# A softmax kernel: the split row moves to the first load, and three tiles become four

## The chip, the cores and the metric

One core of one Trainium2 chip. The metric is device time in microseconds (us) of one execution; the kernel before takes 160.3 us, the median of 5 runs (160.09 to 161.03).

## The reference

The input is 16 x 1024 rows of 512 float32 numbers, 33.55 MB; the output has the same size. Each row goes through a softmax at temperature 2:

```python
x_scaled = x / 2.0
x_max = np.max(x_scaled, axis=-1, keepdims=True)
exp_x = np.exp(x_scaled - x_max)
return exp_x / np.sum(exp_x, axis=-1, keepdims=True)
```

## The kernel before, in words

The 16,384 rows are laid on 128 partitions, so each partition has 128 rows of 2 KB. The text calls "a row" one such row on all 128 partitions (256 KB). The rows are cut into nine tiles, `TILES` (line 10): 3, 5, 15, 15, 25, 25, 10, 15 and 15 rows; each has a place in one buffer in on-chip memory, `arena`, which has room for 98 rows. Within a tile a partition's rows are contiguous in DRAM, so a transfer of r rows moves one piece of r x 2 KB per partition.

The fast path leaves out the row's maximum. ScalarE takes exp(0.5 x) in place, one row at a time, and the same instruction sums the row into `stats` (lines 204 and 271). VectorE takes the reciprocal of up to 15 sums (line 166) and multiplies up to 15 rows by theirs (line 169). At the end a count of sums in a safe range (lines 180 to 196) decides whether a slower path with the maximum must run after all; for these inputs it doesn't.

The order of the work is written out by hand, with a semaphore for each hand-over.

- Loads. `early()` (line 153) issues tile 0 on SyncE's queue and tile 1 on ScalarE's queue, ahead of the barrier at the program's start. After the barrier `loads()` (line 157) issues tiles 2 to 6 on ScalarE's queue, back to back: with tiles 0 and 1 these fill the 98 rows of `arena`.
- Late loads. The two last tiles (7 and 8) reuse rows of `arena` whose tiles have been stored. `LATE` names the tiles whose stores must have landed: 0, 1 and 2 for tile 7, and 3 for tile 8. GpSimd issues them (lines 176 to 179). Ahead of both it waits until the exponentials of all rows up to `TURN` = 63 are done.
- Stores. SyncE issues them in the order of the tiles (line 211), each when VectorE's multiplications of that tile are done (`store`, line 135).
- ScalarE takes rows in groups of 5 (`E`; the first group has 3, `HEAD`). TensorE passes on the landing of a tile (line 194) as so many groups in `s_go`, which ScalarE takes one by one (line 140).
- VectorE multiplies up to three groups at a time, in the last tile one group at a time (line 84).

`load()` (line 113) issues a tile as one transfer, except for the tile numbered `SPREAD`: its last row is loaded by itself, in one transfer over 126 partitions and one over the other 2. Tile `SPREAD` therefore has three transfers and a landing count of 48 instead of 16 (line 194). Before, that is tile 1, on ScalarE's queue.

Of the kernel before, what the change touches and what calls it, by code (L numbers as in the profile page):

```python
# [7 lines left out]


TILES = [  # L10
    (3, 0), (5, 3), (15, 8), (15, 23), (25, 38), (25, 63), (10, 88), (15, 0), (15, 15),
]

LATE = {7: (0, 1, 2), 8: (3,)}
ARENA = 98

HEAD = [3]
E = 5

SPREAD = 1  # L20

TURN = 63

LO, HI = 1.0, 1.0e30
G = 64
# [3 lines left out]
def kernel(  # L29
# [61 lines left out]
    ld = [nc.alloc_semaphore(f"ld{t}") for t in range(len(tiles))]  # L91
    s_home = {t: nc.alloc_semaphore(f"s_home{t}") for t in LATE}
    s_near = nc.alloc_semaphore("s_near")
# [19 lines left out]
    def load(eng, t):  # L113
        r = tiles[t][1]
        parts = [(0, P, 0, r)]
        if t == SPREAD:
            parts = [(0, P, 0, r - 1), (0, 126, r - 1, r), (126, P, r - 1, r)]
        for p, q, lo, hi in parts:
            eng.dma_start(  # L119
                out=sb(t)[p:q, lo:hi], in_=dram(xf, t)[p:q, lo:hi]  # L120
            ).then_inc(ld[t], 16)

    stored_by = {u: s_home[t] for t, us in LATE.items() for u in us}
    for t, (_, r, at) in enumerate(tiles):
        over = {u for u, (_, ru, au) in enumerate(tiles[:t]) if at < au + ru and au < at + r}
        assert over <= {u for v, us in LATE.items() if v <= t for u in us}

    def landings(ts):
        return 16 * len(list(ts))
# [27 lines left out]
    def loads():  # L157
        for t in range(2, min(LATE)):
            load(nc.scalar, t)

    def program():
# [13 lines left out]
        nc.gpsimd.memset(ones[:, :], 1.0).then_inc(s_ones, 1)  # L175
        nc.gpsimd.wait_ge(s_exp, starts.index(TURN))
        for t, us in LATE.items():
            nc.gpsimd.wait_ge(s_home[t], landings(us))
# [14 lines left out]
        for t in range(len(tiles)):  # L193
            nc.tensor.wait_ge(ld[t], 48 if t == SPREAD else 16).then_inc(s_go, owner.count(t))
        nc.tensor.wait_ge(s_ones, 1)
# [126 lines left out]
```

## Time and profile before

| | us |
|---|---|
| Median of 5 runs | 160.3 |
| The profiled execution, its own time | 160.91 |
| Its span, first to last instruction | 159.6 |
| ScalarE busy | 80.5 |
| VectorE busy | 73.3 |
| GpSimd busy | 2.2 |
| Loads of tile 0 issued / landed | 0.0 / 5.8 |
| First exponential | 6.36 |
| First and last store issued | 10.34 / 135.62 |
| Late loads issued | 67.77, 93.96 |

The span is what the profile's views cover; the profiled execution's own time has 1.3 us more, which lie around the span, and it was 0.6 us above the median. The 16 DMA engines of the core are shared by three queues: q1 is SyncE's (tile 0 and all stores), q10 ScalarE's (tiles 1 to 6), q0 GpSimd's (tiles 7 and 8). A packet is one piece of a transfer: one partition's share of a tile, and there is one small packet more for each DMA engine that reports the end of its part. In the windows view the DMA share is the time that the packets begun in a window took, over 16 engines; it may lie over 1, as a packet counts in full where it begins.

### The profile page before, as it was taken

To read this page: it belongs to the slowest core of one execution; us is meant where nothing else is said; L and a number is where in the kernel's file an instruction comes from. 1 tells how busy PE (TensorE), PEld (TensorE's weight loads), DVE (VectorE), ACT (ScalarE), POOL (GpSimd) and SP (SyncE) were. 2 spreads that over 40 slices of the span, in tenths; PEclk is the share of its full clock that TensorE was granted. 3 is DMA by queue.
4 is the path that set the end of the run, shared out by engine and by line. 5 is a ranking of instruction groups with operands and counts; after the bars stand their busy time and mean duration, and the time that the engine had idled before them with its cause. 6 is when DMAs were issued, how large, how long until landed. Compare 5 with 4: busy or idle time off the path is not lost. (4 is left out here: it accounts for less than half of the span.)

```text
span 159.6 us, 656 instructions
## 1 busy us (share of the span) xinstructions
PE 0.2 (0%) x2; PEld 0.1 (0%) x2; DVE 73.3 (46%) x29; ACT 80.5 (50%) x257; POOL 2.2 (1%) x8
## 2 busy tenths in 40 slices
PE   0000000000000000000000000000000000000000
PEld 0000000000000000000000000000000000000000
DVE  0056001992980009994007997019389599000000
ACT  0780498696003999401999700799911992000000
POOL 0000000000000000010000010000000001000000
DMA  6999998999789998989899997998999997999994
GB/s 264 385 493 414 444 440 346 516 493 447 318 352 452 441 521 352 511 352 459 377 488 403 459 485 336 441 503 344 467 413 449 411 500 336 475 431 454 408 454 185
DMA packets 2737, 67.11 MB, mean 421 GB/s; under 512 B 305, under 2 KB 305, under 8 KB 689
## 3 DMA queue, kind: packets, MB, share of 16 engines
q1 hardware_dynamic: 1440, 34.34, 50.1%
q10 hardware_dynamic: 1008, 24.90, 37.0%
q0 software_dynamic: 288, 7.86, 11.5%
q14 instruction: 1, 0.00, 0.0%
HBM read 33.55 MB, written 33.55 MB: 420 GB/s over the span
## 5 line engine op out<-in xcount | busy, mean ns | idle before, releaser
L271 ACT ACTIVATE arena<-arena x125 | 76.6, 614 | 46.9 <-ACTq L140 36.6
L169 DVE TENSOR_TENSOR arena<-arena,recip 128x7680 f32<-128x7680 f32 (+3 forms) x13 | 70.3, 5410 | 0.4
L166 DVE RECIPROCAL recip<-stats 128x15 f32<-128x15 f32 (+3 forms) x13 | 2.8, 217 | 62.2 <-ACT arena L271 53.8
L271 ACT ACTIVATION_READ_ACCUMULATOR arena<-arena x125 | 23.4, 187 | 0.0
L200 ACT ACT_TABLE_LOAD x1 | 1.3, 1283 | 5.1 <-issue 5.1
L119 POOL DMA_DIRECT2D arena<-in_x_dram x2 | 1.3, 632 | 90.5 <-DMA out_dram<-arena 90.5
L204 ACT ACTIVATE arena<-arena 128x512 f32<-128x512 f32 x3 | 1.9, 618 | 0.0
L180 POOL TENSOR_SCALAR inside<-stats 128x128 f32<-128x128 f32 x1 | 0.6, 631 | 38.1 <-ACT arena L271 38.1
L204 ACT ACTIVATION_READ_ACCUMULATOR arena<-arena 128x1 f32 x3 | 0.6, 187 | 0.0
L196 PE MATMUL total<-ones,count 128*1 128x1 f32 x2 | 0.2, 164 | 135.9 <-DVE inside L184 135.9
L184 DVE SCALAR_TENSOR_TENSOR inside<-inside,stats 128x128 f32<-128x128 f32 x1 | 0.3, 284 | 0.0
L188 DVE TENSOR_SCALAR flag<-total 1x1 int32<-1x1 f32 x1 | 0.1, 146 | 0.3 <-PE total L196 0.3
L196 PEld LDWEIGHTS total<-ones,count 128*1 128x1 f32 x2 | 0.1, 80 | 135.9 <-DVE inside L184 135.9
L175 POOL MEMSET ones<- 128x1 f32 x1 | 0.1, 99 | 2.2 <-POOLq L37 2.2
L306 POOL MEMSET const-float32-0.0<- 128x1 f32 x1 | 0.1, 105 | 0.2 <-issue 0.2
L306 POOL MEMSET const-bfloat16-1.0<- 128x1 bf16 x1 | 0.1, 108 | 0.0
L306 POOL MEMSET const-uint8-127<- 128x1 uint8 x1 | 0.1, 108 | 0.0
L306 POOL MEMSET const-float32-1.0<- 128x1 f32 x1 | 0.1, 105 | 0.0
L184 DVE DVE_READ_ACCUMULATOR inside<-inside,stats 128x1 f32 x1 | 0.1, 82 | 0.0
## 6 DMA issues: line engine op xcount, KB each, us to landing
out_dram<-arena SPq DMA_DIRECT2D x4, 3840.0 KB, 28.5
arena<-in_x_dram ACTq DMA_DIRECT2D x2, 6400.0 KB, 58.7
out_dram<-arena SPq DMA_DIRECT2D x2, 6400.0 KB, 40.7
arena<-in_x_dram ACTq DMA_DIRECT2D x2, 3840.0 KB, 20.5
arena<-in_x_dram POOLq DMA_DIRECT2D x2, 3840.0 KB, 29.9
arena<-in_x_dram ACTq DMA_DIRECT2D x1, 2560.0 KB, 96.0
out_dram<-arena SPq DMA_DIRECT2D x1, 2560.0 KB, 28.4
out_dram<-arena SPq DMA_DIRECT2D x1, 1280.0 KB, 28.3
```

Of the source, the lines that this page charges most:

```text
L119: eng.dma_start(out=sb(t)[p:q, lo:hi], in_=dram(xf, t)[p:q, lo:hi]).then_inc(ld[t], 16)
L166: nc.vector.reciprocal(out=recip[:, b : b + c], in_=stats[:, b : b + c])._wait_ge(s_exp, ks[-1] + 1).then_inc(s_rec, 1)
L169: nc.vector.tensor_mul(out=arena[:, a : a + c], in0=arena[:, a : a + c], in1=recip[:, b : b + c].unsqueeze(2).to_broadcast([P, c, D]),)._w ...
L175: nc.gpsimd.memset(ones[:, :], 1.0).then_inc(s_ones, 1)
L180: nc.gpsimd.tensor_scalar(out=inside[:, :], in0=stats[:, :], scalar1=LO, scalar2=HI, op0=Alu.max, op1=Alu.min,)._wait_ge(s_exp, len(sizes) ...
L184: nc.vector.scalar_tensor_tensor(out=inside[:, :], in0=inside[:, :], scalar=1.0, in1=stats[:, :], op0=Alu.mult, op1=Alu.is_equal, accum_ou ...
L188: nc.vector.tensor_scalar(out=flag[:, :], in0=total[:, :], scalar1=float(N), scalar2=None, op0=Alu.is_ge,)._wait_ge(s_tot, 1).then_inc(s_f ...
L196: nc.tensor.matmul(total[:, :], lhsT=count[:, :], rhs=ones[:, :], start=True, stop=True)._wait_ge(s_cnt, 2).then_inc(s_tot, 1)
L200: nc.scalar.preload_act_table(Exp)
L204: ins = nc.scalar.activation(out=arena[:, b], in_=arena[:, b], func=Exp, scale=0.5, accum_out=stats[:, b : b + 1],)
L271: ins = nc.scalar.activation(out=data, in_=data, func=Exp, scale=0.5, accum_out=stats[:, r : n_rows - E + 1 + r][:, bass.ds(now, 1)],)
L306: nc = _bacc.Bacc("TRN2", target_bir_lowering=False, num_devices=1)
```

## The change

- Tiles 4, 5 and 6 (25, 25 and 10 rows) become four tiles of 15 rows. There are now ten tiles: 3, 5 and eight times 15. The late tiles are numbers 8 and 9, with the same places in `arena` and the same stores to wait for.
- `SPREAD` is 0: the transfers over 126 and 2 partitions are now the third row of tile 0, on SyncE's queue, and tile 1 is one transfer.
- `TURN` is 83: GpSimd issues its loads after the exponentials of all rows up to 83.

```diff
 TILES = [
-    (3, 0), (5, 3), (15, 8), (15, 23), (25, 38), (25, 63), (10, 88), (15, 0), (15, 15),
+    (3, 0), (5, 3), (15, 8), (15, 23), (15, 38), (15, 53), (15, 68), (15, 83), (15, 0), (15, 15),
 ]
 
-LATE = {7: (0, 1, 2), 8: (3,)}
+LATE = {8: (0, 1, 2), 9: (3,)}
 ARENA = 98
 
 HEAD = [3]
 E = 5
 
-SPREAD = 1
-
-TURN = 63
+SPREAD = 0
+
+TURN = 83
```

## The prediction

> **What bounds the kernel now.** I read the page's totals first, then the DMA queues, then windows of the span, then who waits.
>
> ```profile
> span 159.6 us, 656 instructions
> PE 0.2 (0%) x2; PEld 0.1 (0%) x2; DVE 73.3 (46%) x29; ACT 80.5 (50%) x257; POOL 2.2 (1%) x8
> DMA packets 2737, 67.11 MB, mean 421 GB/s; under 512 B 305, under 2 KB 305, under 8 KB 689
> q1 hardware_dynamic: 1440, 34.34, 50.1%
> q10 hardware_dynamic: 1008, 24.90, 37.0%
> q0 software_dynamic: 288, 7.86, 11.5%
> ```
>
> No compute engine is busy more than half the time, while the three queues' packets took 50.1 + 37.0 + 11.5 = 98.6% of 16 engines' span, 157.4 us. The windows view (columns: length, busy time of PE, PEld, DVE, ACT and POOL, clock, DMA share, GB/s) says where the rest is:
>
> ```profile
> 0.00:1.00 1.00, 0.00 (x0) 0.00 (x0) 0.00 (x0) 0.00 (x0) 0.21 (x4) 1.00 0.00 0
> 1.00:2.00 1.00, 0.00 (x0) 0.00 (x0) 0.00 (x0) 0.00 (x0) 0.00 (x0) 1.00 0.70 246
> ...
> 8.00:156.00 148.00, 0.19 (x2) 0.09 (x2) 73.34 (x29) 77.61 (x252) 1.90 (x3) 1.00 1.01 432
> ...
> 157.50:158.00 0.50, 0.00 (x0) 0.00 (x0) 0.00 (x0) 0.00 (x0) 0.00 (x0) 1.00 0.30 123
> 158.00:158.50 0.50, 0.00 (x0) 0.00 (x0) 0.00 (x0) 0.00 (x0) 0.00 (x0) 1.00 0.14 61
> 158.50:159.00 0.50, 0.00 (x0) 0.00 (x0) 0.00 (x0) 0.00 (x0) 0.00 (x0) 1.00 0.00 0
> ```
>
> 1.3 us are empty at the start (1.0 + 0.3), nothing from 8 to 156, and 159.6 - 1.3 - 157.4 = 0.9 us at the end. At the end 123 GB/s x 0.5 us = 61 KB is two packets of 30,720 bytes and 61 x 0.5 one more: three of the 16 engines start their last packet up to 1 us after the others. So the time is start + packets + last landing, and a compute engine matters only if it lets the queues run dry.
>
> **Price of a packet.** Three windows of the DMA view hold one size each:
>
> ```profile
> q1 hardware_dynamic: 227, 5.99, 86.8%
> ...
> q1 hardware_dynamic: 91, 4.66, 107.6%
> ...
> q10 hardware_dynamic: 65, 0.13, 98.7%
> ```
>
> 144 to 160 us: 195 packets of 30,720 bytes (and 32 end packets) in 0.868 x 16 x 16 = 222 us, 1.138 us each. 120 to 130: 91 of 51,200 bytes in 172.2 us, 1.892 each. 6.05 to 6.40: 65 of 2048 bytes in 5.53 us, 0.085 each. From the two large sizes 1000 bytes cost 36.8 ns, so what doesn't grow with size is 1.138 - 1.131 = 7 ns in the one and 0.085 - 0.075 = 10 ns in the other: I take 8.5 ns. 4.194 MB and 171 packets per engine then make 154.4 + 1.5 = 155.9 us; the 157.4 hold 1.5 us in which packets took longer than their size explains.
>
> **The change, part by part.** *Four tiles of 15 for 25, 25 and 10.* The bytes stay. One load and one store more are 2 x 144 packets (128 pieces and 16 end packets), 18 per engine: 18 x 8.5 ns = +0.15 us. From below, the longer packets (51,200 bytes) might be what stalls: all 1.5 us gone is the end of that side. From above, the same 1.5 us might come again with more, shorter packets. No row ties these 1.5 us to a size: the windows of 12 us with 50 KB loads at work have 418 and 422 GB/s (32 to 56 us), the one from 128 to 140 404 and that from 140 to 152, with nothing but 30,720-byte stores, 422. I take 0, and +-1.5 as ends.
>
> *The rule that speaks against more transfers.* The Trainium skill ("DMA: Bandwidth & Descriptors", section "Anatomy of one DMA") fits a transfer as about 2.0 us fixed plus its bytes; two more transfers would by that cost up to 4 us. The 1.01 of DMA share from 8 to 156 us, across 11 further issues, says that such a fixed part is latency behind other queued packets.
>
> *The split row.* The same 126 + 2 pieces, the same bytes, another queue. The end packets say how it is spread: 20 whole-tile or split loads and stores at 16 would be 320 small packets and one of instructions, but 305 are under 512 bytes. So the two pieces report for 16 engines together (14 with 9 partitions and 2 with one would be an even cut), and some engines get none of this row. That holds on either queue: 0. On SyncE's queue two issues are added; they took 0.67 and 0.24 us on ScalarE's. They end at about 1.4 instead of 0.38; next behind them are the start's barrier, which now has ScalarE arrive at 0.5 instead of 1.5, and store 0, which waits for VectorE until 10.3. The load after the barrier stays at 2.6. ScalarE then issues six loads of 0.46 us instead of five: its table load starts at 5.4 instead of 5.07 and ends at 6.7. Tile 0 lands later: the nine 2048-byte packets now take turns with tile 1's of 10,240 (0.385 us), 9 x 0.47 = 4.2 us from about 2.6, and 0.5 to report: 7.3 instead of 5.8. First exponential and first store are 1 us later. That is hidden twice: 90 further rows of loads lie queued (0.607 us each, 8 x 1.138 / 15: 55 us), and ScalarE idles 6.4 us before tile 2. If that cover were gone it would cost 1 us.
>
> *The tail.* This is where the tiling could show. Up to tile 3 (landed 29.05) nothing moves. While loads and stores are both queued they take turns: 8 x (1.138 + 1.138) = 18.2 us per tile of 15. Tile 4 meets store 1's short packets: 29.1 + 8 x (1.138 + 0.385) = 41.2. Tiles 5 and 6 land at 59.4 and 77.6. A store follows a landing by 18.1 us (tile 3: 29.05 to 47.20). Row 83 is done 9.6 us after tile 6 landed (15 x 0.611 and the hand-over), 87.2: only now GpSimd issues both late loads, instead of 67.77 and 93.96. In the trace the first q0 packets begin 4.0 and 4.5 us after their issue (71.7, 98.5), here 91.5. Three queues share until tile 7 lands at 97; tile 8 lands at about 111.5 and tile 9 18.2 later, 129.7, against 122.97 for the last tile before. From there to the last store took 12.65 us (135.62 - 122.97): now 142.4, its packets at 143.5 (the first load's came 1.07 after issue). Without the last 15 rows (9.1 us) the engines are busy until 158.2 - 9.1 = 149. So 5.5 us of cover stay of the 12 before (136.7 against 148.6): nothing runs dry, cost 0.
>
> *A rule on GpSimd's loads.* The Trainium skill ("SBUF — State Buffer", section "SBUF: two separate sides") says that GpSimd can't write its transfers' descriptors while VectorE holds the port they share; the two loads now fall on the start of an 8.16 us multiplication. By that rule, if it held for this multiplication, they would begin at 95.8 and the last store 4 us later, still 1.4 us inside the cover. Here both earlier loads had packets before the multiplication beside them ended (71.7 against 73.73, 98.54 against 98.75).
>
> **Sum.** +0.15 on a span of 159.6; the profiled execution had 160.91, 0.6 over the median, and I apply the difference to the median: 160.3 + 0.15 = 160.4 to 160.5, taken as 160.45. About 0.3% (0.5 us) is what a measurement can tell from no change, so this forecast is "the same"; its own range is 160.1 to 160.8.
>
> **The rivals.** (1) *Fewer stalls.* If the 1.5 us go with the 50 KB packets, 0.6 to 1.5 us are gained: about 159.5. For it: packets longer than their size exist. Against: no window of large packets is slower than one of small ones. It decides from 0.65 us saved.
>
> (2) *The late loads starve the tail* (slower). One gate, row 83, and both loads behind it. If the last store comes more than 5.5 us later than worked out, the engines stand idle and each further us costs one; 2 us beyond is 162.3. For it: cover shrinks from 12 to 5.5 us and GpSimd's lag has only been seen as 4.0 and 4.5. Against: tile 9's own lag lies behind tile 8's 18 us.
>
> (3) *The row's relief is lost* (slower). If SyncE's pieces go to other engines than ScalarE's did, an engine that was spared gets its 8 packets back: 8 x 0.085 = 0.68 us; if it is one of the three last, 161.1. For it: only three engines set the end. Against: other transfers show no difference between the queues.
>
> **How the numbers follow.** Forecast 0.55; (1) 0.18; (2) 0.10; (3), with other slips of the three last engines by up to a packet (1.138), 0.17. Faster 0.18, same 0.55, slower 0.27. The range runs from the middle of (1) to past (3), 159.5 to 161.6, leaving out the deep half of (1) and most of (2).
>
> **What would show it.** 3025 packets (2737 + 288); DMA share near 1 from 8 to 156; queues' sum about 157.5 us; first exponential near 7.4; late loads both near 87; last store near 142. A share under 0.9 anywhere between 100 and 150 shows (2); a last-packet lag over 1.5 us shows (3); a packet sum under 156.8 shows (1). I am wrong if the packets' extra time depends on their size.

## The result and the profile after

The changed kernel takes 159.95 us (median of 34 runs, 159.83 to 160.54), the kernel before 160.28 (64 runs beside them). The ratio is 0.9979, with a 95% interval of 0.9971 to 0.9987: 0.33 us, or 0.2%, faster. That is less than the 0.3% bound of the prediction, but it is clear of no change, and the forecast was +0.15 us; 159.95 lies below the range given with the sum (160.1 to 160.8), and inside the wider one that takes in the rivals (159.5 to 161.6). Of some kernels below a part of the executions, called long, takes 162.7 to 168.5 us; the ratios leave these out, so their counts are given beside them.

The page of the changed kernel, totals, queues and one group of part 5:

```profile
span 158.6 us, 657 instructions
...
DMA packets 3024, 67.11 MB, mean 423 GB/s; under 512 B 336, under 2 KB 336, under 8 KB 720
...
q1 hardware_dynamic: 1728, 34.34, 50.5%
q10 hardware_dynamic: 1008, 24.90, 37.0%
q0 software_dynamic: 288, 7.86, 11.5%
...
L204 ACT ACTIVATE arena<-arena 128x512 f32<-128x512 f32 x3 | 1.9, 618 | 9.2 <-ACTq L140 9.2
```

The packets took 99.0% of 158.6, 157.0 us per engine, against 157.4 before. So the 288 further packets are there (18 per engine, priced at +0.15 us), and the sum is 0.4 us lower all the same. The first exponential now waits 9.2 us for tile 0. The timeline has the times (start, length, engine, line):

```profile
0.00 1.18 SPq L119 DMA_DIRECT2D arena<-in_x_dram  x3
0.12 5.14 ACTq L119 DMA_DIRECT2D arena<-in_x_dram  x7
...
5.29 1.28 ACT L200 ACT_TABLE_LOAD   x1 [5.29 <-issue]
15.76 0.63 ACT L204 ACTIVATE arena<-arena 128x512 f32<-128x512 f32 x1 [9.18 <-ACTq L140]
...
19.73 0.38 SPq L137 DMA_DIRECT2D out_dram<-arena  x1
```

The first exponential is at 15.76 (6.36 before, 7.4 predicted), the first store at 19.73 (10.34 before). The windows of the changed kernel show that the queues never run dry, and how it ends (columns as in the prediction; the last two are DMA share and GB/s):

```profile
8.00:156.00 148.00, 0.19 (x2) 0.09 (x2) 73.22 (x27) 79.01 (x256) 1.89 (x3) 1.00 1.00 431
...
156.00:156.50 0.50, 0.00 (x0) 0.00 (x0) 0.00 (x0) 0.00 (x0) 0.00 (x0) 1.00 1.28 553
156.50:157.00 0.50, 0.00 (x0) 0.00 (x0) 0.00 (x0) 0.00 (x0) 0.00 (x0) 1.00 1.00 430
157.00:157.50 0.50, 0.00 (x0) 0.00 (x0) 0.00 (x0) 0.00 (x0) 0.00 (x0) 1.00 0.00 0
157.50:158.00 0.50, 0.00 (x0) 0.00 (x0) 0.00 (x0) 0.00 (x0) 0.00 (x0) 1.00 0.01 0
```

A packet of a last store is 30,720 bytes: 553 GB/s x 0.5 us are 9 of them, 430 x 0.5 are 7. All 16 engines begin their last packet between 156.0 and 157.0. Before, three began theirs between 157.5 and 158.5. The small packets by which an engine reports its end say the same: before, 13 of the last 16 fall between 157.6 and 158.15 and three after that, the last at 159.2; after, all 16 fall between 157.3 and 158.05. So most engines end at nearly the same time in both, and the difference of these two executions lies in how far the last ones are behind; this distance is called the lag below. (The profiled execution before was 0.6 us above its median, the one after at 159.9 on it, so the spans differ by 1.0 and the medians by 0.33. No execution at the median of the kernel before was profiled, so how much of the 0.33 us is lag is not measured directly.)

### The profile page after: what moved, and what is told of

Same layout as the page of the kernel before. It is cut to its first block, busy times and chain, and to the rows that moved or that the text cites. A ratio compares the mean times of both kernels' runs of the same rounds, so it can differ in the third digit from the quotient of the medians.

```text
span 158.6 us, 657 instructions
## 1 busy us (share of the span) xinstructions
PE 0.2 (0%) x2; PEld 0.1 (0%) x2; DVE 73.2 (46%) x27; ACT 80.3 (51%) x257; POOL 2.2 (1%) x8
## 2 busy tenths in 40 slices
DMA packets 3024, 67.11 MB, mean 423 GB/s; under 512 B 336, under 2 KB 336, under 8 KB 720
## 5 line engine op out<-in xcount | busy, mean ns | idle before, releaser
L169 DVE TENSOR_TENSOR arena<-arena,recip 128x7680 f32<-128x7680 f32 (+2 forms) x12 | 70.2, 5847 | 0.4
L166 DVE RECIPROCAL recip<-stats 128x15 f32<-128x15 f32 (+2 forms) x12 | 2.7, 224 | 62.7 <-ACT arena L271 44.9
```

Source lines behind the costliest of these rows:

```text
L166: nc.vector.reciprocal(out=recip[:, b : b + c], in_=stats[:, b : b + c])._wait_ge(s_exp, ks[-1] + 1).then_inc(s_rec, 1)
L169: nc.vector.tensor_mul(out=arena[:, a : a + c], in0=arena[:, a : a + c], in1=recip[:, b : b + c].unsqueeze(2).to_broadcast([P, c, D]),)._w ...
```

## The experiments

Each kernel was timed against the kernel before on the same chip; the four groups ran on four chips (11, 5, 14 and 13, in this order). The edits of kernels with tiles of 15 rows are shown against the changed kernel, those of the others against the kernel before. *Relief* is what the split row brings to engines that get none of its 2 KB packets. Theory A: the tiles bring the gain. Theory B: the moved row does, by delaying the first exponential and the first store.

### The parts apart

**New tiles and gate, split row left in tile 1 on ScalarE's queue.**

```diff
-SPREAD = 0
+SPREAD = 1
```

> The new tiles and gate, with the split row left in tile 1 on ScalarE's queue. Theory A (the saving is the tiles': packets of 51,200 bytes stall or leave three engines behind): 159.95 us, all of the 0.33 us. Theory B (the saving is the split row's, which delays the first exponential to 15.8 us): 160.3 to 160.45, that is no saving, and the first exponential at 6.4 us again.

Measured: eight executions of 13 between 159.88 and 159.97, ratio 0.9982 (0.9968 to 0.9996), and five between 166.5 and 168.5. The tiles and the gate have the whole gain without the moved row, and with it a danger that nobody had expected: 7 us in 5 of 13.

**Old tiles and gate, split row in tile 0 on SyncE's queue.**

```diff
-SPREAD = 1
+SPREAD = 0
```

> The old tiles and gate, with the split row in tile 0 on SyncE's queue. Theory A: 160.3 us, no saving although the first exponential comes at about 15.8 us. Theory B: 159.95, all of the saving. Both parts of it would be half each, about 160.1, if the two add.

Measured: 161.02 us, ratio 1.0040 (1.0017 to 1.0064). Theory B falls: alone, the moved row is a loss of 0.8 us by the medians. The first store is at 19.7, as in the changed kernel, and the end of its profile shows the cost:

```profile
156.50:157.00 0.50, 0.00 (x0) 0.00 (x0) 0.00 (x0) 0.00 (x0) 0.00 (x0) 1.00 1.42 614
157.00:157.50 0.50, 0.00 (x0) 0.00 (x0) 0.00 (x0) 0.00 (x0) 0.00 (x0) 1.00 0.43 184
157.50:158.00 0.50, 0.00 (x0) 0.00 (x0) 0.00 (x0) 0.00 (x0) 0.00 (x0) 1.00 0.01 0
158.00:158.50 0.50, 0.00 (x0) 0.00 (x0) 0.00 (x0) 0.00 (x0) 0.00 (x0) 1.00 0.29 123
158.50:159.00 0.50, 0.00 (x0) 0.00 (x0) 0.00 (x0) 0.00 (x0) 0.00 (x0) 1.00 0.14 61
```

No packet begins between 157.5 and 158.0 but end packets, and then three do (123 x 0.5 and 61 x 0.5 GB/s x us, two and one): 13 engines are through, three are about a packet and a half behind.

**No split row, new tiles.**

```diff
-SPREAD = 0
+SPREAD = -1
```

> The new tiles with no split row at all: ten tiles, one transfer each. If the relief of the two spared engines (8 packets of 2 KB, 0.68 us each) matters with the new tiles, the time is 0.4 to 0.7 us over that of the new tiles with the split, 160.4 to 160.6; if the end is set by other engines, it is 0.1 us under it (9 packets of 0.0085 us fewer on the others), 159.85.

Measured: six of 14 executions between 160.07 and 161.17, ratio 1.0028 (1.0007 to 1.0048); the other eight took 162.8 to 168.4. So the relief counts in the short executions (about 0.7 us against the new tiles with the split row in tile 1). The size isn't firm: the same kernel on another chip, in the last group, has a ratio of 1.0001, which leaves 0.3 us for the relief.

**No split row, old tiles.**

```diff
-SPREAD = 1
+SPREAD = -1
```

> The old tiles with no split row. By the trace of before one of the three engines that end last is of those spared by the split, so without it the time would be up to 0.7 us over the kernel before: 160.9 to 161.0. If the spared engines don't set the end: 160.2.

Measured: 160.81, ratio 1.0031 (1.0016 to 1.0046), none over 161.2. The split row is worth 0.5 to 0.6 us to the kernel before.

**What a long execution is.** The windows of a profiled long one (168.1 us), of the new tiles with no split row:

```profile
156.00:158.00 2.00, 0.00 (x0) 0.00 (x0) 0.00 (x0) 0.00 (x0) 0.00 (x0) 1.00 1.11 476
158.00:160.00 2.00, 0.00 (x0) 0.00 (x0) 0.00 (x0) 0.00 (x0) 0.00 (x0) 1.00 0.22 92
160.00:162.00 2.00, 0.00 (x0) 0.00 (x0) 0.00 (x0) 0.00 (x0) 0.00 (x0) 1.00 0.21 92
162.00:164.00 2.00, 0.00 (x0) 0.00 (x0) 0.00 (x0) 0.00 (x0) 0.00 (x0) 1.00 0.18 77
164.00:166.00 2.00, 0.00 (x0) 0.00 (x0) 0.00 (x0) 0.00 (x0) 0.00 (x0) 1.00 0.07 31
```

From 158 on three of 16 engines work alone (3 / 16 = 0.19), for 7 us. The DMA view of its stretch from 58 to 72 us, where loads and stores take turns:

```profile
q1 hardware_dynamic: 98, 2.92, 52.0%
q10 hardware_dynamic: 109, 2.86, 47.3%
```

and of the same stretch of the changed kernel:

```profile
q10 hardware_dynamic: 114, 3.01, 50.0%
q1 hardware_dynamic: 112, 2.95, 48.8%
```

Stores (q1) are 2.92 MB / 30,720 = 95 packets in 0.520 x 16 x 14 = 116.5 us, 1.23 us each; in the changed kernel 96 in 109.3, 1.14 each. Loads are 1.14 in both (105.9 us for 93; 112 for 98). So in this stretch only stores are slowed, and the packets of the whole trace say by how much: 50 of the 1024 store packets of 30,720 bytes took over 1.3 us (at most 1.76), together 22.8 us more than the usual 1.138 each. That is 7.6 us for each of three engines, and three engines end 7 us late. The changed kernel's trace has no store packet over 1.3 us.

### Relief, gate and length of packets

**The third row of tile 0 loaded apart, but by one transfer over 128 partitions** (the wait for tile 0 is 32): a late first store with no relief.

```diff
-            parts = [(0, P, 0, r - 1), (0, 126, r - 1, r), (126, P, r - 1, r)]
+            parts = [(0, P, 0, r - 1), (0, P, r - 1, r)]
```

> The changed kernel with the third row of tile 0 still loaded apart on SyncE's queue, but by one transfer over all 128 partitions: the delay of the first exponential to about 15 us stays, the relief of the engines spared by the 126 and 2 pieces is gone. If the delay is what keeps the 15-row tiles from executions of 166 to 168 us, none of them is seen here and the time is 160.5 to 160.7 (159.95 + 0.68 of relief). If the relief is what does it, about half the executions are at 165 or above again.

Measured: 159.98 (159.84 to 160.11), ratio 0.9976 (0.9958 to 0.9994), no long execution in 12. The delay is shorter than expected: the first exponential is at 12.11 instead of about 15, the first store at 16.1. So the long ones stay away without the relief, and the delay is what is left (no kernel with an early first store and tiles of 15 ran in this group). The relief's 0.68 us, which I had expected to be missing, is not: with a late first store it has no worth that can be measured here.

**The gate back at row 63.**

```diff
-TURN = 83
+TURN = 63
```

> The changed kernel with the gate of the late loads at row 63 again: GpSimd's loads are issued when store 2 and store 3 have landed, at about 70 and 84 us, instead of 81 to 84. If the saving comes from late loads that no longer run beside 50 KB stores, or from the gate, the time moves by 0.3 us or more towards 160.3. If the gate only uses up cover, it stays at 159.95 within 0.15.

Measured: 160.00, ratio 0.9975 (0.9958 to 0.9992). With a late first store the gate does nothing that can be measured. No kernel had tiles of 15, an early first store and the gate at row 63.

**Tiles of 30 and 30, split row in tile 1.**

```diff
-    ... (25, 38), (25, 63), (10, 88), ...
+    ... (30, 38), (30, 68), ...
...
-TURN = 63
+TURN = 68
```

The late tiles are numbers 6 and 7 here.

> Two tiles of 30 rows in place of 25, 25 and 10, split row in tile 1 as before: 144 x 2 packets fewer than before, the longest now 61,440 bytes. If long packets stall (theory A): 160.5 or more. If packets cost by their number alone (8.5 ns each, 18 fewer per engine): 160.1. If the two are equal: 160.3.

Measured: 159.94 (159.65 to 160.62, and one of 162.83), ratio 0.9966 (0.9947 to 0.9985). The kernel with longer packets is not slower: the form of theory A by which packets of 51,200 bytes stall falls.

**Tiles of 20, 20 and 20, split row in tile 1, gate at 63.**

```diff
-    ... (25, 38), (25, 63), (10, 88), ...
+    ... (20, 38), (20, 58), (20, 78), ...
```

> Three tiles of 20 rows in place of 25, 25 and 10, split row in tile 1 and gate at row 63 as before: the same number of transfers and packets, the longest 40,960 bytes. If the length of a packet is what costs (theory A): between the two kernels, 160.1. If not the length but the number of tiles, or the exact size of 15 rows, does it: 160.3.

Measured: 160.12, ratio 0.9985 (0.9969 to 1.0002). Between the two kernels as expected, though the interval doesn't tell it from the kernel before; and after the tiles of 30 the length can't be the reason. Nor is it the number of packets: 2448 (tiles of 30), 2736 (20) and 3024 (15) give 159.94, 160.12 and about 159.92. What the tiles of 15 and of 30 have that 25, 25 and 10 lack, these runs do not show.

### The late first store by itself

SyncE waits for a landing ahead of its first store; no transfer is changed.

```diff
+        nc.sync.wait_ge(ld[2], 16)
         for t in range(len(tiles)):
             store(nc.sync, t)
```

**New tiles, no split row, wait for tile 2.**

> The new tiles with no split row, where 8 of 14 executions took 162.8 to 168.4 us, and SyncE waits for the landing of tile 2 (about 17.5 us) before it issues store 0. No transfer is changed, only the first store comes at 17.6 instead of 10.3. If a late first store is what keeps the long executions away: none over 161, median 159.9 to 160.1. If it is the apart-loaded row itself (its short packets on SyncE's queue): about half the executions at 165 or above, as without the wait.

Measured: 160.19 (159.82 to 160.74), ratio 0.9992 (0.9977 to 1.0007), first store at 16.6, no long execution in 12, where 8 of 14 were long without the wait. (That was on another chip; on a third, in the last group, 2 of 12 were.) The median is a little over the expected 160.1, and no gain over the kernel before is shown. The stores of the new tiles without and with the wait (the split row in tile 1 in the first, none in the second; first and last start):

```profile
L137 SPq DMA_DIRECT2D out_dram<-arena x10: 332/332/342, 11.0 to 148.4; - x10
...
L137 SPq DMA_DIRECT2D out_dram<-arena x10: 332/332/424, 16.6 to 137.9; - x10
```

**The kernel before with the same wait.**

> The kernel before (25, 25 and 10, split row in tile 1), with the same wait of SyncE for tile 2's landing ahead of store 0. If the late first store is what made the old tiles slower with the split row in tile 0 (161.0): 160.9 to 161.1. If that loss came from the split row leaving ScalarE's queue: 160.2 to 160.3, no change.

Measured: 161.03, ratio 1.0028 (1.0009 to 1.0047), against 161.02 with the row moved: eight of the 12 executions lie between 160.89 and 161.16, the other four between 160.07 and 160.40. The late first store by itself accounts for the moved row's loss with the old tiles.

**New tiles, no split row, wait for tile 3.**

```diff
+        nc.sync.wait_ge(ld[3], 16)
```

> As the first of these, but SyncE waits for tile 3's landing: first store at about 27 instead of 17.6 us. If any sufficiently late first store will do: 159.9 to 160.1 and none over 161. If it has to fall at a certain place against the loads, executions over 162 are back. If the cover is used up by it, the last store comes after the queue has run dry and each us of it costs one; the loads end earlier instead, so I expect no such cost.

Measured: 159.95, ratio 0.9978 (0.9965 to 0.9991), first store at 25.8, the last already at 128.9 (136.0 in the changed kernel). 15 us of delay cost nothing, with neither split row nor relief.

**Tiles of 30, no split row, wait for tile 2** (the gate at row 68, as in the kernel with tiles of 30 above).

> Two tiles of 30 rows, no split row, and the wait for tile 2: the fewest packets of all kernels here (2304). By packets alone 0.3 us under the kernel before, 159.9; if the last engines' lag is smaller too, 159.6 to 159.7, under both kernels. If long packets with a late first store lag as the old tiles did with the split row in tile 0: 160.6 or more.

Measured: 163.32, ratio 1.0173 (1.0146 to 1.0201): a miss, and the only kernel whose queue ran dry. Its windows:

```profile
147.00:149.00 2.00, 0.00 (x0) 0.00 (x0) 1.95 (x3) 1.56 (x6) 0.34 (x1) 1.00 0.72 307
149.00:151.00 2.00, 0.00 (x0) 0.00 (x0) 2.00 (x1) 0.00 (x0) 0.29 (x1) 1.00 0.21 92
151.00:156.00 5.00, 0.19 (x2) 0.09 (x2) 1.00 (x4) 0.00 (x0) 0.00 (x0) 1.00 0.81 344
```

The last store is issued at 151.7, when the engines have been mostly idle for about 3 us (a DMA share of 0.07 to 0.29 in each microsecond from 148 to 152): rival 2 of the prediction, in another kernel. With the same tiles and gate, the split row and no wait the time was 159.94, so a delay that costs nothing with tiles of 15 can use up the cover with larger ones.

### What is behind the long executions

Three kernels run beside each other: no split row and no wait once more, the same with the 15-row tiles taken from DRAM in another order, and from last to first. Only the place in DRAM differs.

```diff
-        b, r, _ = tiles[t]
+        b, r, _ = tiles[[0, 1, 2, 6, 3, 7, 4, 8, 5, 9][t]]
```

```diff
-        b, r, _ = tiles[t]
+        b, r, _ = tiles[[0, 1, 9, 8, 7, 6, 5, 4, 3, 2][t]]
```

> The new tiles with no split row and no wait, once more and on the chip of the next three: about half the executions between 162 and 169 us again, the others at 160.0 to 161.2. If none is over 162 here, the long executions belong to a chip or a time and not to the kernel.

> The same, with the eight tiles of 15 rows drawn from DRAM in another order, so that the store of a tile and the load two tiles on, which run side by side, lie mostly one block (3.9 MB) apart instead of two (7.9 MB); queues, sizes and times of issue are as in the control. If the long executions come from the two streams' distance in DRAM: their share or their length changes clearly (none over 162, or all). If they come from the engines' turns alone: about half between 162 and 169, as in the control.

> The same, with the eight tiles of 15 rows taken from the last DRAM block to the first: the distance is two blocks still, with the load behind the store. If the distance counts whatever its sign: as the control. If its sign counts too: a clear change here. By the engines' turns alone: as the control.

Measured: 2 of 12 long (167.3 and 167.6), 6 of 12 (163.1 to 168.0) and 6 of 14 (166.4 to 167.8); the others at 160.0 to 161.2. The long ones have the same length in all three, and neither order removes them: the distance between the two streams in DRAM isn't needed for them. Their share varies by itself (8 of 14 and 2 of 12 for one and the same kernel), so the shares tell nothing finer.

**Split row in tile 1, new tiles, wait for tile 2.**

```diff
-SPREAD = 0
+SPREAD = 1
...
+        nc.sync.wait_ge(ld[2], 16)
```

> The new tiles with the split row in tile 1 on ScalarE's queue (5 of 13 executions at 166.5 to 168.5), and SyncE's wait for tile 2 ahead of store 0. If the late first store is all that the change's move of the split row brings: none over 161 and 159.9 to 160.0, the time of the changed kernel.

Measured: 159.98 (159.78 to 160.15), ratio 0.9981 (0.9972 to 0.9989), no long execution in 12, beside 14 of 38 in the three kernels without the wait on the same chip. In time and in long executions the wait stands in for the moved row.

Taken together: tiles of 15 with a first store at 10 to 11 us had 27 long executions of 65; with a first store at 16 us or later none in 94. What makes the few engines' stores slow then stays open. Missing relief isn't needed (5 of 13 were long with it), nor is one order of the tiles in DRAM. But all 65 executions with an early first store had both the tiles of 15 and the gate at row 83; the kernels with other tiles and an early first store (25, 25 and 10, or 20, or 30 rows, one long execution of 162.83) had the gate at 63 or 68. Which of the two is needed isn't shown.

The lag is what the times follow in the short executions too. There are 14 profiles of short executions with full queues. In 13 of them, 13 of the 16 engines have reported their end by 157.7 to 158.2 us, and the last one at 158.05 to 159.7, while the times run from 159.84 to 161.39. (In the 14th, of the first other order in DRAM, 13 are through at 158.6 and the last at 158.8.)

## Why the prediction was wrong, and where it was right

- *What bounds the kernel* held: the DMA share is 1.00 from 8 to 156 us, and all kernels but one keep the queues full.
- *The end* was the wrong step. The sum took "0.9 us at the end" as fixed and saw only packets, stalls and cover as terms. The lag of the last engines, which that part had itself read off (three engines up to 1 us behind), is the term that the change moved: in the profiles from a last packet begun by 158.5 to one begun by 157.0, and from 0.9 us at the end to 0.4 (158.6 less 1.2 empty at the start less 157.0). The packets' sum, forecast at +0.15, fell by 0.4; three engines that are 1.1 us late make 0.2 us of such a mean over 16. A step "four tiles of 15: 0 for stalls" that names no effect on the lag can't give it. Why these tiles have less lag stays open.
- *Four tiles, +0.15 us* by 18 packets per engine: their number is right (3024, predicted 3025), their price can't be seen; kernels with 18 packets per engine fewer or more don't differ in that order.
- *The rule of 2 us per transfer* would have had up to 4 us: the result is -0.33, the trace's side of it was right.
- *The split row* was mis-sized: tile 0 was to land at 7.3, the first exponential to come at 7.4; it came at 15.76. The short packets of 2048 bytes take turns not only with tile 1's of 10,240 bytes but, from 6.1 us on, with tile 2's of 30,720, where one turn takes 0.085 + 1.138 = 1.2 us. In the trace they begin between 4.2 and 13.8 us, 90 of the 128 before 7 us; the last ones hold up tile 0. That it is hidden held by itself (the queues stay full), but "1 us later, cost 0" missed that the time of the first store decides on the lag: with old tiles it costs 0.8 us by the medians, with tiles of 15 no long execution is seen.
- *The tail*: the last store came at 136.0, not 142.4, because the stores' late begin lets the loads go ahead: the late loads were issued at 80.94 and 84.41 instead of 87. Without that delay the sum nearly fits: in a short execution of the new tiles with no split row and no wait the late loads are issued from 88.0 and the last store at 143.9. Rival 2 did not happen here, but its price, one us for each us of dry queues, fits where it did: about 3 us mostly idle with the wait and tiles of 30, and 163.32 against 160.23 for the kernel before beside it.
- *The rule on GpSimd's loads* did not hold for this multiplication. The changed kernel's timeline, of GpSimd and of VectorE:

```profile
80.94 0.73 POOL L119 DMA_DIRECT2D arena<-in_x_dram  x1 [78.53 <-ACT arena L271]
...
80.95 8.16 DVE L169 TENSOR_TENSOR arena<-arena,recip 128x7680 f32<-128x7680 f32 x1
```

  The DMA view from 84 to 86.5 us has 13 q0 packets, while VectorE multiplies until 89.1. The first of them begins at 85.9, 4.9 us after the issue (4.0 and 4.5 before).
- *Rival 1*, fewer stalls with the 50 KB packets, had the sign and, with 0.33 us, about half of the low end of its 0.6 to 1.5, but not its reason: tiles of 30 are as fast. *Rival 3* asked the right question, which engines are last; the row's relief is worth 0.3 to 0.7 us with an early first store and not measurable with tiles of 15 and a late one.

## What to carry to other kernels

In a kernel whose transfers are never idle, the time is that of the last of 16 engines: read how many packets begin in the last 2 us, and treat that lag as a term of the sum. A change that only shifts when the first store begins may leave the queues full and still move that lag in either direction, so it is to be measured together with the tiling it goes with. Look at every execution, not at the median alone: a kernel with 8 good executions of 13 and a median of 159.95 is not the same as one with 34 of 34.

## What was not expected of the hardware

Two or three of 16 DMA engines can fall 6 to 8 us behind the others in some executions of one program: their stores take longer (1.23 us against 1.14 in the mean over all engines from 58 to 72 us) while loads keep their 1.14. It was seen only with tiles of 15 rows, the gate at row 83 and a first store before 11 us (27 of 65 executions), apart from one execution of 162.83 us with tiles of 30 that was not profiled, and in none of 94 with 6 us or more of delay on one queue. A delay of 7 us made the kernel with 25, 25 and 10 rows 0.8 us slower by the medians.
